# Attention's transposes one unit later, scores in two banks, and inputs loaded once or in place, in a hybrid encoder layer on one core

## The chip, the core and the metric

The kernel runs on one NeuronCore of a Trainium2 chip. The core has a matrix engine (TensorE, PE in the profile; its weight loads are PEld), a vector engine (VectorE, DVE), a scalar engine (ScalarE, ACT), GpSimd (POOL) and a sync engine (SyncE, SP). SP issues nearly all transfers of this kernel, and 16 DMA engines carry them out. Work on chip uses the SBUF (128 partitions); matmuls write into the PSUM, which here is cut into eight banks of 128 x 512 f32. The metric is the device time of one execution in microseconds (us): less is better. The engines run side by side, each through its own queue in order, and wait for each other through semaphores.

## What is computed

Two sequences (1024 and 2048 tokens of 1024 channels) each get 16 meta tokens in front and go through one encoder layer with shared weights. All of it is f32; the kernel splits every f32 operand of a large matmul into a high and a low part (`xh`, `xl`) and sums three products.

```python
xn = _rmsnorm(h, g_pre)
proj = xn @ w_in + b_in
na_q, na_k, na_v, na_z, ml_qk, ml_v, ml_z, ml_o, ml_g, mg = split(proj)
ya = (neighbourhood_attention(na_q, na_k, na_v, na_rpb) * silu(na_z)) @ w_a
yb = (mlstm_branch(ml_qk, ml_v, ml_g, ml_o, conv_w, head_g) * silu(ml_z)) @ w_b
ga, gb = split(sigmoid(mg))
y = (ga * ya + gb * yb) @ w_out
return h + _rmsnorm(y, g_post)
```

The attention puts the tokens on a grid of 64 columns. A query sees a window of 8 rows and 16 columns and the 16 meta tokens; the scores get a bias from a table, then softmax, then the product with v. There are 8 heads of 64 channels.

## The kernel before

TensorE's order is written out by hand: two generators yield pieces of work with a cost in us, and a small loop (`run`) takes dense pieces until they cover the cost of the sparse piece before. The order of the other engines' queues is set by a scheduler that plays the program through a timeline of its own, so an edit can move instructions there that the diff does not name.

*Dense* work (`dense`, following `PLAN`) is the input projection in half sequences and then six final blocks (`final`), each for 512 tokens. A final block has two halves. In the first, for each of eight column groups, 48 products take the branch outputs of the attention and the mLSTM, held as `yh` and `yl` (8 slices `k` of 128 channels, 0 to 3 attention, 4 to 7 mLSTM), with the merged weights; VectorE applies the gates (L1467, L1469) and the result is split into `mh` (L1470, ScalarE) and `mlo` (L1471, VectorE). In the second half 768 products form the output projection, which `final_out` normalises and adds to the input (L1571) during the next block. Weights come as `whi` and `wlo` through four buffers each (`wpump`, L243), issued when a buffer is free.

The branch outputs stand in DRAM (`YA`, `YB`). The generator `yload` fetches those of the next block: it is started in the last job of the projection (the first block) or in the second half of the block before (all others), and advanced one step at a time between TensorE's pieces. For each slice it waits until that slice is done (`self.done`), loads it into a buffer `yr` (L1418, 256 KB) of the pool tag `st`, which it shares with the gates' tiles and the projection's output tiles, and splits it two slices later: ScalarE copies it to `yh` (L1405), VectorE writes the rest to `yl` (L1406). The tiles `yh` and `yl` take their slots from the tags `xh` and `xl` (two each), as do `mh`, `mlo` and the projection's inputs.

*Sparse* work (`sparse`) is, in turn, the mLSTM and the attention (`na`) of the first sequence, then of the second (`STEPS`). Attention goes by blocks of eight grid rows, pairs of heads and heads: 16 heads' turns for the first sequence, 32 for the second, each with four *units*, one for each block of 16 query columns (`cb`). `na_prep` fetches and splits the inputs of the next head's turn in six steps between the units of this one: the queries `qr` (by `twice`, the same 64 rows to partitions 0 to 63 and again to 64 to 127), the keys `kr` (twice as well), the meta keys, the values `vr` and the gate `zt`. From `qr` it builds `stk`, whose lower 64 partitions are the high part of the queries and whose upper 64 the low part: ScalarE copies all 128 partitions (L824), VectorE overwrites the upper 64 with the difference (L827).

A unit passes through four stages, one for each yield in an iteration of `na`'s loop:

- `na_scores`: two products (L849, L850) into one PSUM bank `sc`; VectorE adds the bias and takes the extreme (L853, `mx`); ScalarE takes the exponential into `prb` (L857).
- `na_scale`: VectorE divides by the sum (L865, L866).
- `na_turn`: four transposes on TensorE (L874) into a bank `tr`; ScalarE and VectorE write the high and low part to `pts` (L876, L877).
- `na_out`: four products with v (L886) into a bank `sm`; ScalarE and VectorE add the three parts into `yg` (L890, L892). After the last unit of a pair of heads `yg` is gated (L894) and written to `YA` (L895), and the slice is marked done.

In iteration `u` the loop runs scores and scaling of unit `u`, the transposes of unit `u - 1` and the products with v of unit `u - 2`. The PSUM banks are `BANKS = dict(pj=3, tr=2, sc=1, sm=2)`: `pj` belongs to the dense work, `sc` holds the scores of attention and mLSTM, `sm` the products with v and several products of the mLSTM.

Of the kernel before, what the change touches and what calls it, by code (L numbers as in the profile page):

```python
# [9 lines left out]
F32 = mybir.dt.float32  # L10
# [7 lines left out]
P = 128  # L18
# [102 lines left out]
class K:  # L121
# [3 lines left out]
    def __init__(self, tc, ins, outs):  # L125
        self.tc, self.nc = tc, tc.nc
        self.xs = []
        self.i, self.o = ins, outs
        self.wreq, self.wraw, self.wrdy, self.wout = deque(), deque(), deque(), 0
        self.wseen, self.wkept, self.xkept = set(), {}, {}  # L130
        self.rwait = {}
        self.xput, self.turn, self.last = deque(), 0, None
        self.hold, self.early = deque(), True
# [601 lines left out]
    def na(self, s, rts):  # L735
# [3 lines left out]
        with tc.tile_pool(name=f"na{s}{rts[0]}", bufs=1, side="right", reuse_waits="tile") as np_:  # L739
# [18 lines left out]
            ready = {}  # L758
            for u in range(len(units) + 2):
                if u < len(units):  # L760
# [14 lines left out]
                yield A_NA  # L775
                if 1 <= u <= len(units):
                    self.na_turn(np_, ready[u - 1], rows)
                    if u < len(units) and cb >= 2:
                        next(prep, None)
                yield A_NA  # L780
                if u >= 2:
                    self.na_out(np_, ready.pop(u - 2), s)
                yield A_NA
# [9 lines left out]
    def na_prep(self, np_, s, rows, heads, j):  # L793
# [8 lines left out]
        qb = self.qB[hh]  # L802
        self.twice(qr, self.NQ[s][pr], h0, rt * 512)
        sv = stk.rearrange("p b t -> p (b t)")
# [18 lines left out]
        yield  # L823
        nc.scalar.activation(sv, qr, AF.Copy)  # L824
        yield
        nc.scalar.activation(qb[0:64], stk[0:64].bitcast(F32), AF.Copy)
        nc.vector.tensor_tensor(sv[64:128], qr[64:128], sv[64:128].bitcast(F32), op=ALU.subtract)  # L827
        yield
# [11 lines left out]
    def na_scores(self, np_, unit, rows):  # L840
# [5 lines left out]
        N, kc, g0 = ns * 32, KC0[cb], (5, 1, 0)[typ]  # L846
        sc = self.psum("sc", [P, 512])
        so = sc[:, :N].rearrange("p (a b) -> p a b", b=32)
        nc.tensor.matmul(so, stk[:, cb, :], kd[:, :ns, kc:kc + 32], start=True, stop=False)  # L849
        nc.tensor.matmul(so, qb[:, cb, :], self.kx[hh][:, :ns, kc:kc + 32], start=False, stop=True)  # L850
        pr_ = np_.tile([P, 512], F32, name="prb", bufs=2)
        mx = np_.tile([P, 1], F32, name="mx", bufs=3)
        nc.vector.tensor_tensor_reduce(  # L853
            out=so, in0=so, in1=gt[:, g0:g0 + ns, c0:c0 + 32],
            op0=ALU.add, op1=ALU.min, scale=-1.0, scalar=3.0e38, accum_out=mx)
        sm = np_.tile([P, 1], F32, name="sm", bufs=3)
        nc.scalar.activation(pr_[:, :N].rearrange("p (b a c) -> p b a c", b=4, c=8),  # L857
# [537 lines left out]
    def yload(self, s, b):  # L1395
# [5 lines left out]
        todo = deque()  # L1401

        def split():
            k, yr = todo.popleft()
            nc.scalar.activation(yh[:, k], yr, AF.Copy)  # L1405
            nc.vector.tensor_tensor(yl[:, k], yr, yh[:, k].bitcast(F32), op=ALU.subtract)  # L1406
            self.yk.add(k)

        for k in (4, 5, 6, 7, 0, 1, 2, 3):
            need = ("ml", s) if k > 3 else ("na", s, b, k)  # L1410
            if need not in self.done:
                while todo:
                    split()
                    yield
                while need not in self.done:
                    yield "wait"
            yr = fp.tile([P, n], F32, name="yr", tag="st", bufs=4)
            nc.sync.dma_start(yr, self.YA[s][b][k][:, :] if k < 4 else self.YB[s][k - 4][:, b * n:(b + 1) * n])  # L1418
            todo.append((k, yr))
            if len(todo) == 3:  # L1420
                split()
                yield
        while todo:
            split()
            yield

# [271 lines left out]
```

## Time and profile before

| | |
|---|---|
| time, median of 3 runs | 2843.53 us (2842.91 to 2847.38) |
| the profiled execution's own time | 2845.39 us |
| its span in the profile | 2843.6 us |
| its mean granted TensorE clock | 0.994 |
| DMA traffic over the span | 661.42 MB, 233 GB/s on average |

The page of the profile gives each engine's busy time and the costliest groups of instructions. A group's row reads: line, engine, operation, output <- inputs, count, busy time, mean of one, and the idle time before it with what ended it. Views of the trace narrow this: the waits (who waited for whom, in us, times and the longest), stretches (busy time of each engine between two points, with the granted clock as a share of full speed and the DMA engines' busy share), one line's instructions (shortest, median and longest duration in ns, then the first and last start), the timeline, and the chain of work that ended last. Times within the span count from its start. L numbers are lines of the kernel before.

### The profile page before, as it was taken

The page shows a single profiled execution, that of the slowest core. Times are in us where ns is not written, and L with a number is a line of the kernel's source. Part 1 is how long each engine was busy: PE and PEld are TensorE (multiplying, and loading weights), DVE is VectorE, ACT ScalarE, POOL GpSimd, SP SyncE. Part 2 cuts the span into 40 slices and gives each one's busy share as a digit, 9 for nine tenths or more (in the row PEclk, how much of TensorE's full clock was granted, in tenths as well). Part 3 has the DMA queues.
Part 4 walks back from the last instruction along what each step waited for, and adds up shares of the span by engine and source line. Part 5 has one row for each costly group of instructions (what it writes and reads, how often), then busy time and mean ns, then how long its engine had stood idle before and what let it go on. Part 6 is the DMA issues. An engine that isn't in the chain of part 4 may idle for free.

```text
span 2843.6 us, 49257 instructions
## 1 busy us (share of the span) xinstructions
PE 2795.7 (98%) x17312; PEld 2488.8 (88%) x17312; DVE 1796.3 (63%) x4931; ACT 1306.4 (46%) x3135; POOL 16.1 (1%) x103
## 2 busy tenths in 40 slices
PE   9999999999999999999999999999999999999998
PEld 8998898999899988888988888888888988889898
DVE  5233678576456654456667566474679888787854
ACT  5122546444444443355455555453455554545421
POOL 0000000000000000000000000000000000000000
PEclk9999999999999999999999999999999999999999
DMA  9554768765966554685656776656679999897875
GB/s 373 186 186 178 261 210 300 252 196 165 343 210 192 169 173 131 189 281 181 210 176 224 251 274 193 185 171 180 196 239 355 308 308 279 286 291 258 290 259 193
DMA packets 382120, 661.42 MB, mean 233 GB/s; under 512 B 51664, under 2 KB 200608, under 8 KB 381872
## 3 DMA queue, kind: packets, MB, share of 16 engines
q1 hardware_dynamic: 380752, 655.58, 69.7%
q0 software_dynamic: 1120, 2.69, 0.4%
q8 instruction: 137, 2.24, 0.3%
q14 instruction: 111, 0.91, 0.1%
HBM read 455.90 MB, written 202.22 MB: 231 GB/s over the span
## 4 chain that ended last, share of the span: by engine, by line
PE 85%; DMA 8%; DVE 5%; ACT 1%; issue 1%; SPq 0%; DVEq 0%; ACTq 0%
PE pj L155 15%; PE pj L156 14%; PE pj L157 14%; PE pj L577 6%; PE pj L578 6%; PE pj L579 6%; PE pj L1499 3%; PE pj L1497 3%; PE pj L1498 3%; PE sm L886 3%; PE tr L874 2%; DMA wlo<-wl 1%; DMA um<-ud 1%; PE sm L157 1%; PE sc L849 1%; PE sm L156 1%
## 5 line engine op out<-in xcount | busy, mean ns | idle before, releaser
L155 PE MATMUL pj<-xh,whi 128*128 128x512 f32 (+1 forms) x1792 | 705.7, 394 | 0.9 <-ACT whi L250 0.9
L156 PE MATMUL pj<-xl,whi 128*128 128x512 f32 (+1 forms) x1792 | 689.5, 385 | 0.1
L157 PE MATMUL pj<-xh,wlo 128*128 128x512 f32 (+1 forms) x1792 | 688.2, 384 | 0.3 <-DVE wlo L251 0.3
L577 PE MATMUL pj<-whi,xh 128*128 128x256 f32 (+3 forms) x1576 | 451.2, 286 | 4.4 <-DMA whi<-wh 2.9
L578 PE MATMUL pj<-wlo,xh 128*128 128x256 f32 (+3 forms) x1576 | 445.1, 282 | 0.8 <-DMA wlo<-wl 0.8
L579 PE MATMUL pj<-whi,xl 128*128 128x256 f32 (+3 forms) x1576 | 444.6, 282 | 0.0
L157 PEld LDWEIGHTS pj<-xh,wlo 128*128 128x128 f32 x1792 | 337.2, 188 | 72.1 <-DVE wlo L251 0.5
L155 PEld LDWEIGHTS pj<-xh,whi 128*128 128x128 f32 x1792 | 337.7, 188 | 60.5 <-ACT whi L250 1.7
L156 PEld LDWEIGHTS pj<-xl,whi 128*128 128x128 f32 x1792 | 338.0, 189 | 56.9 <-issue 1.0
L577 PEld LDWEIGHTS pj<-whi,xh 128*128 128x128 f32 (+1 forms) x1576 | 294.5, 187 | 6.4 <-DMA whi<-wh 3.1
L578 PEld LDWEIGHTS pj<-wlo,xh 128*128 128x128 f32 (+1 forms) x1576 | 294.3, 187 | 2.1 <-DMA wlo<-wl 1.1
L579 PEld LDWEIGHTS pj<-whi,xl 128*128 128x128 f32 (+1 forms) x1576 | 294.3, 187 | 0.9
L1497 PE MATMUL pj<-whi,mh 128*128 128x256 f32 x768 | 220.9, 288 | 4.2 <-DMA whi<-wh 2.4
L1499 PE MATMUL pj<-whi,mlo 128*128 128x256 f32 x768 | 217.5, 283 | 1.1 <-DVE mlo L1471 1.1
L1498 PE MATMUL pj<-wlo,mh 128*128 128x256 f32 x768 | 217.5, 283 | 0.1
L857 ACT ACTIVATE prb<-sc,mx 128x384 f32<-128x384 f32 (+2 forms) x192 | 119.8, 624 | 204.2 <-DVE mx L853 193.2
L877 DVE TENSOR_TENSOR pts<-tr,pts 96x512 fp32r<-96x512 f32 (+2 forms) x192 | 131.5, 685 | 75.8 <-ACT pts L876 74.3
L876 ACT ACTIVATE pts<-tr 96x512 fp32r<-96x512 f32 (+2 forms) x192 | 113.9, 593 | 114.8 <-PE tr L874 113.5
L155 PE MATMUL pj<-yh,whi 128*128 128x512 f32 x384 | 155.9, 406 | 0.0
L156 PE MATMUL pj<-yl,whi 128*128 128x512 f32 x384 | 152.2, 396 | 0.0
L157 PE MATMUL pj<-yh,wlo 128*128 128x512 f32 x384 | 152.2, 396 | 0.0
L1497 PEld LDWEIGHTS pj<-whi,mh 128*128 128x128 f32 x768 | 146.3, 190 | 6.5 <-ACT mh L1470 2.3
(271 smaller groups left out, 5049.4 us busy)
## 6 DMA issues: line engine op xcount, KB each, us to landing
whi<-wh SPq DMA_DIRECT2D x176, 512.0 KB
wlo<-wl SPq DMA_DIRECT2D x176, 512.0 KB
wraw<-wu SPq DMA_DIRECT2D x64, 512.0 KB
wh<-whi SPq DMA_DIRECT2D x64, 512.0 KB
wl<-wlo SPq DMA_DIRECT2D x64, 512.0 KB
gt<-st SPq DMA_DIRECT2D x96, 256.0 KB
tg<-gt SPq DMA_DIRECT2D x96, 256.0 KB
xt<-xt SPq DMA_DIRECT2D x32, 512.0 KB
```

The source lines that it names most:

```text
L155: mm(out, ah, bh, start=start, stop=False)
L156: mm(out, ah, bl, start=False, stop=False)
L157: mm(out, al, bh, start=False, stop=stop)
L577: nc.tensor.matmul(o, xh, wh, start=k == 0, stop=False)
L578: nc.tensor.matmul(o, xh, wl, start=False, stop=False)
L579: nc.tensor.matmul(o, xl, wh, start=False, stop=k == KT - 1)
L857: nc.scalar.activation(pr_[:, :N].rearrange("p (b a c) -> p b a c", b=4, c=8), sc[:, :N].rearrange("p (a b c) -> p b a c", b=4, c=8), AF.E ...
L876: nc.scalar.activation(pts[:ks, :, 0, :], pt[:ks], AF.Copy)
L877: nc.vector.tensor_tensor(pts[:ks, :, 1, :], pt[:ks], pts[:ks, :, 0, :].bitcast(F32), op=ALU.subtract)
L1497: nc.tensor.matmul(o, mh[:, k, xs], wh, start=k == 0, stop=False)
L1498: nc.tensor.matmul(o, mh[:, k, xs], wl, start=False, stop=False)
L1499: nc.tensor.matmul(o, ml[:, k, xs], wh, start=False, stop=k == KT - 1)
```

## The change

The change has four parts.

1. *Queries once.* `qr` is loaded only to partitions 0 to 63. ScalarE copies these 64 to `stk`, and VectorE takes the difference from partitions 0 to 63 and writes it to the upper 64.
2. *Transposes and v products one unit later.* In iteration `u` the loop now runs the transposes of unit `u - 2` and the products with v of unit `u - 3`, with one iteration more at the end. `prb` has three buffers and `mx` and `sm` (the sums) four.
3. *Scores in two banks in turn.* The scores of every other unit go to a bank of the tag `sm`, the rest to `sc` as before.
4. *Branch outputs in place.* `yload` loads a slice straight into its place in `yl`; ScalarE copies from there to `yh`, and VectorE subtracts in place. All slices that are done at the start are loaded at once; then come six empty steps, then one split a step. Slices that are not done yet are kept in `late` and loaded, with two empty steps, as soon as they are done.

```diff
@@ na
-            for u in range(len(units) + 2):
+            for u in range(len(units) + 3):
...
-                if 1 <= u <= len(units):
-                    self.na_turn(np_, ready[u - 1], rows)
+                if 2 <= u <= len(units) + 1:
+                    self.na_turn(np_, ready[u - 2], rows)
...
-                if u >= 2:
-                    self.na_out(np_, ready.pop(u - 2), s)
+                if u >= 3:
+                    self.na_out(np_, ready.pop(u - 3), s)
@@ na_prep
-        self.twice(qr, self.NQ[s][pr], h0, rt * 512)
+        nc.sync.dma_start(qr[0:64], self.NQ[s][pr][h0:h0 + 64, rt * 512:(rt + 1) * 512])
...
-        nc.scalar.activation(sv, qr, AF.Copy)
+        nc.scalar.activation(sv[0:64], qr[0:64], AF.Copy)
...
-        nc.vector.tensor_tensor(sv[64:128], qr[64:128], sv[64:128].bitcast(F32), op=ALU.subtract)
+        nc.vector.tensor_tensor(sv[64:128], qr[0:64], sv[0:64].bitcast(F32), op=ALU.subtract)
@@ na_scores
-        sc = self.psum("sc", [P, 512])
+        self.turns = not self.turns
+        sc = self.psum("sc" if self.turns else "sm", [P, 512])
...
-        pr_ = np_.tile([P, 512], F32, name="prb", bufs=2)
-        mx = np_.tile([P, 1], F32, name="mx", bufs=3)
+        pr_ = np_.tile([P, 512], F32, name="prb", bufs=3)
+        mx = np_.tile([P, 1], F32, name="mx", bufs=4)
@@ yload
+        def load(k):
+            nc.sync.dma_start(yl[:, k].bitcast(F32), self.YA[s][b][k][:, :] if k < 4 else self.YB[s][k - 4][:, b * n:(b + 1) * n])
+            todo.append(k)
+
         def split():
-            k, yr = todo.popleft()
-            nc.scalar.activation(yh[:, k], yr, AF.Copy)
-            nc.vector.tensor_tensor(yl[:, k], yr, yh[:, k].bitcast(F32), op=ALU.subtract)
+            k = todo.popleft()
+            nc.scalar.activation(yh[:, k], yl[:, k].bitcast(F32), AF.Copy)
+            nc.vector.tensor_tensor(yl[:, k], yl[:, k].bitcast(F32), yh[:, k].bitcast(F32), op=ALU.subtract)
             self.yk.add(k)
 
+        late = []
         for k in (4, 5, 6, 7, 0, 1, 2, 3):
-            need = ("ml", s) if k > 3 else ("na", s, b, k)
-            if need not in self.done:
-                while todo:
-                    split()
-                    yield
-                while need not in self.done:
-                    yield "wait"
-            yr = fp.tile([P, n], F32, name="yr", tag="st", bufs=4)
-            nc.sync.dma_start(yr, self.YA[s][b][k][:, :] if k < 4 else self.YB[s][k - 4][:, b * n:(b + 1) * n])
-            todo.append((k, yr))
-            if len(todo) == 3:
+            if (("ml", s) if k > 3 else ("na", s, b, k)) in self.done:
+                load(k)
+            else:
+                late.append(k)
+        for _ in range(6):
+            yield
+        while todo or late:
+            while late and (("ml", s) if late[0] > 3 else ("na", s, b, late[0])) in self.done:
+                load(late.pop(0))
+                for _ in range(2):
+                    yield
+            if todo:
                 split()
                 yield
-        while todo:
-            split()
-            yield
+            else:
+                yield "wait"
```

In the order of TensorE's instructions, which is fixed by hand, the counts and shapes of all products are the same before and after; the units of attention are shifted by one against each other as described. SP issues 48 transfers fewer. The queues of VectorE, ScalarE and SP are put in another order by the scheduler from the first attention on.

More of the change, by code (lines that the diff above doesn't have):

```diff
@@ L131, in __init__ @@
         self.rwait = {}
-        self.xput, self.turn, self.last = deque(), 0, None
+        self.xput, self.turn, self.last, self.turns = deque(), 0, None, False
         self.hold, self.early = deque(), True
@@ L855, in na_scores @@
             op0=ALU.add, op1=ALU.min, scale=-1.0, scalar=3.0e38, accum_out=mx)
-        sm = np_.tile([P, 1], F32, name="sm", bufs=3)
+        sm = np_.tile([P, 1], F32, name="sm", bufs=4)
         nc.scalar.activation(pr_[:, :N].rearrange("p (b a c) -> p b a c", b=4, c=8),
```

## The prediction

> **What bounds the kernel now.** I read the engine rows of the page first, then TensorE's waits, then where they fall, then one of them in order of time.
>
> ```profile
> PE 2795.7 (98%) x17312; PEld 2488.8 (88%) x17312; DVE 1796.3 (63%) x4931; ACT 1306.4 (46%) x3135; POOL 16.1 (1%) x103
> ```
>
> TensorE is busy for 2795.7 us of a span of 2843.6 us. The diff changes no matmul's count or shape, so nearly everything that it can win lies in the other 47.9 us. The waits of TensorE say whose they are (waited for, us in total, times, longest):
>
> ```profile
> PE tr L874 <- DVE prb L866: 12.3, 7, 3.3
> PE sc L849 <- ACT prb L857: 5.9, 4, 3.0
> PE pj L577 <- DMA whi<-wh: 2.9, 1, 2.9
> ...
> PE pj L1497 <- DMA whi<-wh: 2.4, 2, 1.6
> PE pj L1497 <- ACT mh L1470: 1.8, 1, 1.8
> ```
>
> The first two rows are the two that the change touches. Seven transposes waited for the scaled probabilities (12.3 us) and four score products for the exponentials to leave the only `sc` bank (5.9 us): 18.2 us. The stretches say where (start:end, length, then busy time and count of PE, PEld, DVE, ACT, POOL, then clock, DMA share, GB/s):
>
> ```profile
> 2100.00:2700.00 600.00, 579.31 (x3654) 519.46 (x3653) 497.93 (x1156) 311.40 (x731) 2.04 (x4) 0.99 0.92 299
> 710.00:1150.00 440.00, 436.34 (x2756) 394.50 (x2756) 245.02 (x626) 188.19 (x400) 1.74 (x16) 0.99 0.64 204
> ```
>
> Attention runs in both. In the first attention (second row) VectorE is busy 56% and TensorE loses 3.7 us in all. While the second attention runs beside the final blocks (first row), VectorE is busy 83%, the DMA engines 92%, and TensorE loses 20.7 us.
>
> One wait of the transposes, from the timeline (start, length, engine, line; TensorE's two rows first):
>
> ```profile
> 2641.17 0.64 PE L886 MATMUL sm<-pts,vt 104*128 104x256 f32 x4
> ...
> 2648.25 1.07 PE L874 MATMUL tr<-ident,prb 128*104 128x128 f32 x4 [3.32 <-DVE prb L866]
> ...
> 2644.36 0.26 DVE L892 TENSOR_TENSOR yg<-sm,yg 64x128 f32<-64x128 f32 x1
> ...
> 2645.74 1.41 DVE L1571 SCALAR_TENSOR_TENSOR yo<-yo,nwy,xres 128x512 f32<-128x512 f32 x2 [0.56 <-DMA xres<-x_sample]
> 2647.07 0.68 DVE L1469 TENSOR_TENSOR tg<-tg 128x512 f32<-128x512 f32 x1
> 2647.67 0.43 DVE L866 TENSOR_SCALAR prb<-prb,sm 128x416 f32<-128x416 f32 x1
> ```
>
> VectorE works its queue in order. The scaling (L866) stands behind a residual add (L1571) that waits for a transfer, and behind the final block's own operations. VectorE is not short of time over the stage (102 us free of 600), it is late in bursts, and the transposes are due too early to ride one out.
>
> **Transposes and v products one unit later.** A unit is one of the four column blocks of a head, and the stage holds:
>
> ```profile
> 2100.00:2700.00 600.00, 38.63 (x100) 19.09 (x100) 0.99 0.92 299
> ```
>
> This is the same stretch for the second score product (L850) alone: 100 units in 600 us, 6.0 us a unit. The transposes now come one unit, 6.0 us, later behind the same scaling. The longest wait is 3.3 us, so a burst like those of before is over 2.7 us ahead of the due time. Gain 12.3 us. The PSUM evacuation after the transposes and the v products move with them, so their distance stays.
>
> **Scores in two banks.** A score bank is now written again after two units and not one; for the scores in `sc` the longest wait of 3.0 us is covered by 6.0 more. Gain 5.9 us.
>
> **The clock.** Waits cost more than themselves. The transposes' waits in three stretches of a hundred us (from 2100, 2500 and 2200 on, one row of each), beside the longest of 3.0 and 3.3 us above (at 2573 and 2648); and then stretches of 20 us around the long ones:
>
> ```profile
> PE tr L874 <- DVE prb L866: 2.9, 2, 2.4
> PE tr L874 <- DVE prb L866: 2.8, 1, 2.8
> PE tr L874 <- DVE prb L866: 1.7, 1, 1.7
> ```
>
> ```profile
> 2155.00:2175.00 20.00, 17.09 (x78) 13.67 (x77) 17.31 (x37) 9.40 (x18) 0.00 (x0) 0.91 1.05 324
> 2515.00:2535.00 20.00, 17.21 (x79) 13.91 (x78) 16.64 (x37) 7.55 (x16) 0.51 (x1) 0.91 1.06 336
> 2560.00:2580.00 20.00, 17.04 (x119) 16.27 (x118) 15.46 (x34) 12.23 (x29) 0.00 (x0) 0.91 0.92 315
> 2640.00:2660.00 20.00, 16.68 (x78) 13.91 (x77) 17.66 (x41) 6.36 (x15) 0.00 (x0) 0.91 0.96 303
> 2280.00:2300.00 20.00, 18.29 (x92) 14.97 (x91) 18.16 (x41) 6.84 (x17) 0.00 (x0) 1.00 1.01 326
> ```
>
> The first four (waits of 2.4 to 3.3 us) have a granted clock of 0.91, the last (1.7 us) of 1.00. At 0.91, 20 us have lost 0.09 x 20 = 1.8 us. Four of them: 7.2 us, which goes with the waits. [...]
>
> **What the new place costs.** Two things can come back.
>
> The odd units' scores now share the two `sm` banks with the v products. In order of allocation that is product, scores, product, product, scores: half of the products and half of the scores must find the product of about one unit earlier evacuated, where a product used to have two units. In the burst above, a product issued at 2641.17 is out of its bank when L892 ends at 2644.62, 3.5 us later and inside 6.0; that is the lower end, nothing. The upper end is the nearest row of a wait at one unit's distance, the scores' own 5.9 us with one clock loss, 7.7 us. Half of the units are affected, so I take half of 5.9: 3.0 us.
>
> The v product keeps its distance to its operand, and the pause that TensorE made at the transposes no longer holds it back. Its smallest margin in the trace:
>
> ```profile
> 2195.76 0.68 DVE L877 TENSOR_TENSOR pts<-tr,pts 128x512 fp32r<-128x512 f32 x1
> ...
> 2197.63 0.60 PE L886 MATMUL sm<-pts,vt 128*128 128x256 f32 x3
> ```
>
> The operand is ready at 2196.44, 1.2 us ahead. If each of the four largest transposes' waits (3.3, 2.8, 2.4, 1.7) met such a margin, 2.1 + 1.6 + 1.2 + 0.5 = 5.4 us would return; if VectorE has caught up by then, nothing. I take the middle, 2.7 us.
>
> **Queries once.** 48 of these transfers go, one for each head:
>
> ```profile
> qr<-nq SPq DMA_DIRECT2D x96, 128.0 KB
> ```
>
> That is 48 issues fewer on SP's queue and 6.3 MB. TensorE waited for no query, so I count nothing; the upper end is a gain of 3 us, the weights' wait of 2.9 us in the third row of the waits, which falls where attention starts and the queue is crowded. ScalarE's copy and VectorE's subtraction stay one operation each over 512 columns.
>
> **Branch outputs in place.** The 48 loads, copies and subtractions (below, of 128x512 f32, 256 KB each) remain in the same shapes:
>
> ```profile
> L1406 DVE TENSOR_TENSOR yl<-yr,yh x48: 673/684/694, 2101.5 to 2730.9; 128x512 fp32r<-128x512 f32 x48
> ```
>
> New is that up to eight loads (2.1 MB) are issued together, then six steps pass, then one split a step; before, loads ran three ahead. They write a slot of `yl` whose last reader, the block before, is past, so SP does not wait long for it. 2.1 MB at 299 GB/s is 7.0 us in front of the next weights. Weights have four buffers, so a transfer is issued two to three units ahead. Eight of the 48 copies below belong to a block and fill the first half of its time; 48 span five and a half blocks, so a block takes about 118 us, a unit of weights 7.4 us and the lead is 15 to 22 us. The second row is the slowest weight transfer that I saw in the chain of waits:
>
> ```profile
> L1470 ACT ACTIVATE mh<-tg x48: 612/632/636, 2140.1 to 2788.2; 128x512 fp32r<-128x512 f32 x48
> ...
> 2300.01 8.80 DMA whi<-wh
> ```
>
> 8.8 + 7.0 = 15.8 us just fits. I count nothing; the case that it doesn't is a rival.
>
> The tail: the last attention row is now finished one unit later, with 84 output products left behind it instead of 156 (one every 0.12 us by the first two rows below: 9.9 us of cover). From the last v product's evacuation (third row) to the end of the last split, which the row of L1406 has starting at 2730.9, the trace has 7.3 us:
>
> ```profile
> 2729.73 0.28 PE L1499 MATMUL pj<-whi,mlo 128*128 128x256 f32 x1
> 2729.85 0.28 PE L1497 MATMUL pj<-whi,mh 128*128 128x256 f32 x1
> ...
> 2724.27 0.60 DVE L892 TENSOR_TENSOR yg<-sm,yg 64x128 f32<-64x128 f32 x2 [1.27 <-ACT yg L890]
> ```
>
> and the last eighth of that block's inputs is read only after 21 products of 512 columns more. So nothing; without that cover the last block would start some 7 us late.
>
> **Sum.** 12.3 + 5.9 + 7.2 - 3.0 - 2.7 = 19.7 us off the profiled execution's 2845.4 us, which stands 1.9 us above the median of the three runs (2843.5). From the median: 2824 us. Its own range is 2815 to 2831: nothing given back and 3 us for the queries, or both costs of the new place at their upper ends (7.7 + 5.4 us).
>
> **The rivals.**
>
> VectorE takes the time back. It is at 83%, and with TensorE earlier by 20 us the same bursts meet the next consumers: v products, final blocks' `pj` banks, `mh` and `mlo` at the head of the output products, which already show 1.8 us. For it speaks the 83%; against it, that 102 us of VectorE are free and each burst is shorter than the new distance. If three quarters of the 25.4 us return, 6 us remain: 2837 us.
>
> The burst of loads makes the kernel slower. From the point where a weight transfer behind the eight loads takes more than the lead of 15 us and upward, TensorE waits in each of the six final blocks. With a DMA share of 0.92 to 1.06 that is near. Three us and a clock loss of 1.8 us in each block are 29 us: 2843.5 - 19.7 + 29 = 2853 us. Against it: only 2.4 us of waits for weights are seen now in the final blocks.
>
> The change doesn't do what it says: VectorE's order is set anew by due times, and scaling that is due later may be queued later, so that the transposes are late as before. Then only the scores' 5.9 us and one clock loss go: 2836 us. Against it: the unit's own scores to exponential chain has no later due time.
>
> More than I forecast: the weights' waits (2.9 and 2.4 us) and those of `mh` (1.8 us) go too, with one clock loss each for the first and last, for less traffic and a VectorE that is ahead, some 10 us: 2814 us.
>
> **How the numbers follow.** Forecast 0.58, VectorE 0.14, due times 0.07, loads 0.15, more 0.06. The measurement of this kernel can tell 0.2%, 5.7 us, from no change: below 2837.8 is faster. Forecast and more are faster, and a third of the 0.21 of the two middle cases: 0.71. The rest of these is no change (0.14), and the loads are slower: 0.15. The range reaches from the extra gain to a mild form of the burst: 2814 to 2846.
>
> **What would show it.** Right: the rows of transposes waiting for L866 and scores waiting for L857 gone or under 3 us together, the busy time of PE unchanged but for the clock, no 20 us stretch at 0.91 between 2100 and 2700. Bank sharing wrong: waits of scores or of the v products' first matmul for VectorE's L892. VectorE: new waits at L886, L155 or L1497 of the same total. Loads: L1497 or L155 waiting for weights by more than 2.4 us in total. Queries: fewer bytes by 6.3 MB. The prediction fails if these waits go and the span does not follow them.

## The result and the profile after

The changed kernel takes 2836.33 us (median of 7 runs, 2834.41 to 2840.43), the kernel before on the same chip 2847.38 us (7 runs, 2842.91 to 2854.93). The ratio is 0.9961 with a 95% interval of 0.9943 to 0.9979: faster, by about 11 us. The forecast was 19.7 us less. Direction and range held, the size did not. The profiled execution took 2834.41 us, with a span of 2832.6 us against 2843.6 us before, so the profiles show the same 11.0 us.

Engine rows of the page, after (busy time, share of the span, instructions):

```profile
PE 2790.1 (99%) x17312; PEld 2484.0 (88%) x17312; DVE 1791.9 (63%) x4931; ACT 1307.6 (46%) x3135; POOL 16.2 (1%) x103
```

TensorE's busy time fell by 5.6 us (2795.7 to 2790.1) with the counts unchanged: that is the granted clock, 0.996 on average against 0.994. What remains of the span beside it fell by 5.4 us, from 47.9 to 42.5. The waits of TensorE, after (waited for, us in total, times, longest; lines of this kernel are one to six higher than before):

```profile
PE sm L887 <- ACT prb L858: 6.1, 5, 2.4
PE sm L157 <- DVE ktl L1155: 5.7, 5, 1.9
PE sm L887 <- DVE yg L893: 5.6, 4, 3.0
...
PE sm L850 <- DVE yg L893: 2.5, 4, 1.4
PE pj L1503 <- DMA whi<-wh: 2.1, 2, 1.4
PE sm L850 <- DVE sm L866: 1.9, 1, 1.9
...
PE sm L887 <- ACT kd L829: 1.2, 1, 1.2
```

The rows of the transposes and of the scores waiting for `sc`, 18.2 us, are gone. In their place stand 17.3 us on the two `sm` banks: 12.9 us at the v products (L887: 6.1 + 5.6 + 1.2) and 4.4 us at the odd units' scores (L850: 2.5 + 1.9). The other 4.5 us of the smaller idle time are little rows that came and went: waits for `mh` (1.8), `mlo` (1.1), `kf` (1.2) and two mLSTM rows of products into the score bank (2.6 and 0.8) are gone, one for `ktl` grew from 2.6 to 5.7.

The second attention (start:end, length, busy time and count of PE, PEld, DVE, ACT, POOL, then clock, DMA share, GB/s):

```profile
2100.00:2700.00 600.00, 582.77 (x3719) 523.45 (x3718) 497.93 (x1173) 313.37 (x744) 2.04 (x4) 0.99 0.91 296
```

TensorE loses 17.2 us of the 600 where it lost 20.7. One of the new waits in order of time, from the timeline of the changed kernel:

```profile
2519.67 0.68 DVE L878 TENSOR_TENSOR pts<-tr,pts 128x512 fp32r<-128x512 f32 x1
...
2521.84 0.69 ACT L858 ACTIVATE prb<-sm,mx 128x512 f32<-128x512 f32 x1 [2.22 <-DVE mx L854]
...
2522.68 0.74 PE L887 MATMUL sm<-pts,vt 128*128 128x256 f32 x4 [1.59 <-ACT prb L858]
```

The operand `pts` was ready at 2520.35, more than two us ahead. The product started 0.15 us after the exponential of the scores *of the same iteration* had ended (2522.53): it had been given the `sm` bank in which those scores stood. In every odd iteration a unit's scores and its product both need an `sm` bank and only two exist, so the product must wait either for those scores or for the product of the iteration before. All ten waits of the products (0.2 to 3.0 us) fall in odd iterations and end 0.14 to 0.15 us after the one or the other: five after the exponential of those scores (6.1 us), five after L893 of the product before. The rows that name `kd` (L829) and the sums `sm` (L866) are of the second kind: there too L893 ended 0.15 us before the start, and the instruction named happened to end a little later.

### The profile page after: what moved, and what is told of

Same layout as the page of the kernel before. It is cut to its first block, busy times and chain, and to the rows that moved or that the text cites. A ratio compares the mean times of both kernels' runs of the same rounds, so it can differ in the third digit from the quotient of the medians.

```text
span 2832.6 us, 49099 instructions
## 1 busy us (share of the span) xinstructions
PE 2790.1 (99%) x17312; PEld 2484.0 (88%) x17312; DVE 1791.9 (63%) x4931; ACT 1307.6 (46%) x3135; POOL 16.2 (1%) x103
## 2 busy tenths in 40 slices
DMA packets 378278, 655.11 MB, mean 231 GB/s; under 512 B 50896, under 2 KB 199840, under 8 KB 378032
## 4 chain that ended last, share of the span: by engine, by line
PE 85%; DMA 7%; DVE 5%; ACT 1%; issue 1%; SPq 0%; DVEq 0%; ACTq 0%
PE pj L155 15%; PE pj L156 15%; PE pj L157 15%; PE pj L577 6%; PE pj L578 6%; PE pj L579 6%; PE pj L1503 3%; PE pj L1505 3%; PE pj L1504 3%; PE sm L887 3%; PE tr L875 2%; PE sm L157 1%; DMA wlo<-wl 1%; PE sm L156 1%; PE sm L155 1%
## 5 line engine op out<-in xcount | busy, mean ns | idle before, releaser
L1504 PEld LDWEIGHTS pj<-wlo,mh 128*128 128x128 f32 x768 | 147.0, 191 | 1.7
```

Of the source, the lines that this page charges most:

```text
L1504: nc.tensor.matmul(o, mh[:, k, xs], wl, start=False, stop=False)
```

## The experiments

The runs stand here by question, not in order of time, so an expectation can name a result that is told further down. Each ratio is against runs of the kernel before on the same chip and need not be the quotient of two medians. The spans of single profiled executions scatter by more than the effects looked for, so ratios decide about time and profiles about places. "The attention's waits" are those that begin at 2100 us or later.

### Each part alone

Part 1 alone on the kernel before:

```diff
-        self.twice(qr, self.NQ[s][pr], h0, rt * 512)
+        nc.sync.dma_start(qr[0:64], self.NQ[s][pr][h0:h0 + 64, rt * 512:(rt + 1) * 512])
...
-        nc.scalar.activation(sv, qr, AF.Copy)
+        nc.scalar.activation(sv[0:64], qr[0:64], AF.Copy)
```

> The kernel before with part 1 alone (queries loaded once). Parts 1 and 4 together cost 0.65% when attention is not shifted. Theory A (the loads in place do it, by a burst of splits): this kernel is within 0.2% of before and the transposes wait near 12 us. Theory B (the queries do it, by the new order of the queues): it is slower by 0.4% or more, with 20 us or more of waits of the transposes.

Measured: ratio 1.0013 (0.9996 to 1.0029), no change that can be told. Transposes waited 17.5 us in 8 places in its profile.

Part 4 alone on the kernel before:

```diff
-            nc.scalar.activation(yh[:, k], yr, AF.Copy)
-            nc.vector.tensor_tensor(yl[:, k], yr, yh[:, k].bitcast(F32), op=ALU.subtract)
+            nc.scalar.activation(yh[:, k], yl[:, k].bitcast(F32), AF.Copy)
+            nc.vector.tensor_tensor(yl[:, k], yl[:, k].bitcast(F32), yh[:, k].bitcast(F32), op=ALU.subtract)
...
+        for _ in range(6):
+            yield
```

> The kernel before with part 4 alone (branch outputs loaded in place, all at once). Theory A: slower by 0.4 to 0.7%, with some 20 us or more of waits of the transposes for L866, the added ones around the splits before each final block. Theory B: within 0.2% of before. If neither alone is slower, the two add up only through the order that the scheduler finds for them together.

Measured: ratio 1.0026 (1.0011 to 1.0040), slightly slower. Transposes waited 20.5 us in 10 places.

Parts 1 and 4 together (both edits above):

> Parts 1 and 4 of the change alone (queries once, branch outputs in place), attention's order and banks as before. If these two are neutral, as the prediction has it, the time is that of before within 0.2% (5.7 us) and TensorE's waits of the transposes for L866 and of the scores for the exponential stay near 18 us. If loading all slices at once lets the splits run in a burst that holds up ScalarE and VectorE, those waits grow and the time is above that of before by 3 us or more. If they are a gain of their own, it is below by more than 3 us.

Measured: ratio 1.0065 (1.0042 to 1.0088), 18 us slower. Its waits:

```profile
PE tr L874 <- DVE prb L866: 24.1, 12, 4.6
PE sc L849 <- ACT prb L857: 7.6, 4, 5.3
...
PE pj L1502 <- DMA whi<-wh: 2.8, 2, 2.2
```

Weights are waited for by little more than before in the final blocks (2.8 and, for `wlo`, 0.8 us against 2.4), so delayed weights are not what costs 18 us. The transposes' row doubled (12.3 to 24.1): with these edits the scaling comes later, and as long as the transposes are due early, TensorE pays. Neither part alone explains it, with 0.13% that can't be told from nothing and 0.26%; how the two add up to 0.65% is open.

Part 2 alone:

```diff
-                    self.na_turn(np_, ready[u - 1], rows)
+                    self.na_turn(np_, ready[u - 2], rows)
...
-                    self.na_out(np_, ready.pop(u - 2), s)
+                    self.na_out(np_, ready.pop(u - 3), s)
```

> The kernel before with part 2 alone (transposes and v products one unit later, prb three times). If the shift is the part that gains, as the run with one score bank suggests (0.9973 with parts 1, 2 and 4, against 1.0065 with 1 and 4), the transposes' waits go to under 1 us, the scores still wait for the exponential by 6 to 13 us, and the time is 0.2 to 0.5% below before. If it gains only by repairing what parts 1 and 4 cost, it is within 0.2% of before.

Measured: ratio 0.9985 (0.9973 to 0.9996), some 4 us. Its waits:

```profile
PE sc L849 <- ACT prb L857: 17.1, 11, 5.3
```

The transposes no longer wait, but the scores' wait for their one bank grew from 5.9 to 17.1 us. What was won at one place came back at the next place with little distance.

Part 3 alone:

```diff
-        sc = self.psum("sc", [P, 512])
+        self.turns = not self.turns
+        sc = self.psum("sc" if self.turns else "sm", [P, 512])
```

> The kernel before with part 3 alone (scores in the sc bank and in an sm bank in turn). Question: does sharing the two sm banks cost anything by itself, while TensorE still pauses at the transposes and the distance from the last product with v to its evacuation is 3.2 us as before? If the order of allocation alone costs (two sm banks are too few for one unit's scores and two products), TensorE waits for sm banks by 10 us or more, as in the changed kernel (17.3 us), and the time is about that of before or slower, ratio 1.000 to 1.004. If those waits come from the lag that the shift brings, TensorE waits for sm banks by less than 6 us, the scores' 5.9 us go, the transposes keep 10 to 15 us, and the ratio is 0.996 to 0.9995.

Measured: ratio 1.0007 (0.9991 to 1.0023). The waits came as the second expectation had them, the time as the first: the scores' wait for `sc` went, and nothing was gained. Its waits:

```profile
PE tr L875 <- DVE prb L867: 14.0, 9, 3.4
PE pj L1498 <- ACT mh L1471: 5.9, 1, 5.9
PE sm L887 <- ACT prb L858: 4.1, 4, 1.6
...
PE sm L887 <- ACT yh L1406: 0.8, 1, 0.8
PE sm L887 <- DVE yg L893: 0.8, 1, 0.8
```

At the v products the sharing gave back 5.7 us (4.1 + 0.8 + 0.8) of the 5.9 it saved; the 5.9 us for `mh` are one wait of this execution. With the shift in place it costs 17.3 us. The transposes lie between a unit's scores and its product with v in TensorE's order; here they still stand for 14.0 us, and in that time banks come free.

### The changed kernel with one part taken out

Without part 3, all scores in `sc` again:

```diff
-        self.turns = not self.turns
-        sc = self.psum("sc" if self.turns else "sm", [P, 512])
+        sc = self.psum("sc", [P, 512])
```

> The changed kernel with the scores always in sc: parts 1, 2 and 4. Theory 1 (the 17 us of new waits come from scores and v products sharing the two sm banks): the v products' waits (17 us of new waits, 12.9 of them at the v products) go to under 3 us, the scores' waits for the exponential come back with about 6 us, and the time is 4 to 10 us below the changed kernel. Theory 2 (VectorE is late whatever the banks are): the v products wait as in the changed kernel and the score waits come on top, so the time is 3 us or more above the changed kernel.

Measured: ratio 0.9973 (0.9962 to 0.9984), which can't be told from the changed kernel's 0.9961. The waits of the v products went but for 0.9 us, as the first theory had it. In their place the scores waited 12.7 us in 13 places for `sc`, twice what that theory gave them and not far from what the two `sm` banks cost in the changed kernel (17.3).

Without part 4, the loads of the kernel before:

```diff
-            nc.scalar.activation(yh[:, k], yl[:, k].bitcast(F32), AF.Copy)
+            nc.scalar.activation(yh[:, k], yr, AF.Copy)
```

> The changed kernel with the loading of the branch outputs as before (through st, three loads ahead, splits apart). Theory 3 (the burst of splits, behind loads that land late, holds ScalarE and VectorE in the output products): the three waits of v products in those halves (1.3, 2.6 and 3.0 us) go, and with two clock losses the time is 5 to 10 us below the changed kernel. Theory 1 (only the banks): the waits keep their total of 17 us within 4 us and the time stays within 3 us.

Measured: ratio 0.9976 (0.9963 to 0.9989), and the same waits at the same places:

```profile
PE sm L887 <- ACT prb L858: 8.2, 6, 2.4
PE sm L850 <- DVE yg L893: 7.0, 3, 4.3
```

So part 4 is not the source of the new waits, and the rival of the burst of loads falls a second time. That does not clear late loads as such: they stand in SyncE's queue with part 4 and without it.

### More banks

Scores, transposes and v products of the changed kernel take the banks `sc`, `tr`, `sm`, `tr`, `sm` in turn, so that a bank is written again after five pieces:

```diff
+    def bank(self):
+        self.turns += 1
+        return self.psum(("sc", "tr", "sm", "tr", "sm")[self.turns % 5], [P, 512])
...
-        av = self.psum("sm", [P, 512])
+        av = self.bank()
```

> The changed kernel with the five banks sc, tr, sm, tr, sm given in turn to scores, transposes and v products, so that each bank comes up again after five uses, one and two thirds of a unit. Theory 1 (sharing of two banks within one unit): scores' and v products' waits fall from 17 us to under 5 us, and with the clock losses the time is 12 us or more below the changed kernel (about 2824 us). Theory 2 (VectorE late whatever the banks are): waits of the same sum come at the v products for pts or at the transposes, and the time is that of the changed kernel within 3 us.

Measured: ratio 0.9951 (0.9934 to 0.9968). The five banks are waited for by 0.2 us in all. Now the products' operand is:

```profile
PE sm L890 <- DVE pts L881: 8.8, 3, 3.4
```

The first theory wanted 12 us less than the changed kernel, the second the same time within 3 us with waits at `pts`. The second comes nearer: the two intervals overlap, and the lateness met the next buffer.

The same on the kernel before with part 2 (parts 1 and 4 left out), the edit being those of part 2 and of the banks above:

> The kernel before with part 2 and the five banks in turn, without parts 1 and 4. If the banks were the cause of the new waits and parts 1 and 4 give nothing, the time is at or below that of the changed kernel with five banks (0.995 of before), with no wait for a bank and less than 9 us for pts. If parts 1 and 4 help once attention is shifted, it is above 0.997.

Measured: ratio 0.9948 (0.9928 to 0.9967), the same as with parts 1 and 4, whose cost is hidden once the distances are large. The products' operand is waited for by 0.9 us here. The waits have moved again, to the projection's banks and `mlo`:

```profile
PE pj L1501 <- DVE yo L1529: 4.6, 2, 4.1
...
PE pj L1503 <- DVE mlo L1475: 3.6, 2, 2.9
```

Four buffers in turn (operand of the transposes, score bank, `sm` bank, projection bank) have now been the one that TensorE stands before. That left the question of what makes VectorE and ScalarE late.

### What is late

With the distances grown, both engines also run later behind TensorE: over some 100 units of the second attention the time from the start of a unit's last v product to the end of its evacuation averages 3.2 us before and 3.8 us after. My next theory was that this mean lag makes the new waits, since a pause of TensorE had also been time for VectorE to catch up. The multiplication by the reciprocal of the sum (L866) is 46.3 us of VectorE's work between 2100 and 2700. It goes to ScalarE, on the kernel before and on the changed kernel:

```diff
-        nc.vector.tensor_scalar(pr_[:, :N], pr_[:, :N], sm, None, op0=ALU.mult)
+        nc.scalar.activation(pr_[:, :N], pr_[:, :N], AF.Copy, scale=sm)
```

> The kernel before, only the multiplication by the reciprocal of the sum (L866) goes from VectorE to ScalarE. It takes 46 us of the 600 us from 2100 on off VectorE (83% to 75%) and puts some 50 to 60 us on ScalarE (52% to 61%). If lateness of VectorE is what TensorE waits for, the transposes' waits (12.3 us) fall to 6 us or less and the time falls by 6 to 15 us, ratio 0.995 to 0.998. Rival: ScalarE's own queue (exponentials, copies of four other kinds) is as bursty; the transposes wait as before, now for ScalarE, and the exponentials behind a late multiplication hold the only bank of the scores longer: ratio 0.999 to 1.004.

Measured on the kernel before: ratio 0.9943 (0.9921 to 0.9965), at least as much as the whole change. Its attention's waits:

```profile
PE sc L849 <- ACT prb L857: 7.2, 4, 2.7
...
PE tr L874 <- ACT prb L866: 1.8, 3, 1.0
```

The transposes' waits went from 12.3 to 1.8 us with no distance added. Little of them reappeared: the scores' row went from 5.5 us (of its 5.9, those after 2100) to 7.2. The multiplication itself takes longer there (0.64 against 0.44 us in the median), but it comes sooner when VectorE is behind: from the end of the exponential to the end of the multiplication the slowest ten of some 100 take 3.0 us or more against 4.9, the longest 4.4 against 6.5.

> The changed kernel with the same move of the multiplication to ScalarE. If what remains (17.3 us of waits for sm banks) is the lag of VectorE and ScalarE behind a TensorE that no longer pauses, 46 us less on VectorE should bring the distance from the last product with v to its evacuation from 3.8 us to 3.4 or less and the waits for sm banks to 8 us or less: ratio to the kernel before 0.990 to 0.994. Rival (the banks' order sets the waits, whatever VectorE does): waits stay at 14 to 20 us, ratio 0.995 to 0.998. Second rival: ScalarE becomes the late one (the evacuation begins with ScalarE's copy into yg), waits grow over 20 us, ratio 0.998 to 1.002.

Measured on the changed kernel: ratio 0.9965 (0.9949 to 0.9981), no gain over 0.9961. The lag from product to evacuation fell to 3.2 us as the theory wanted, but 11.9 us of waits for `sm` banks stayed, more than the theory's 8 and less than the first rival's 14, and 1.6 us for the operand came up. The time is what the first rival gave. So the mean lag can explain a part of the waits at most, and nothing of the time; as the cause that theory falls. The longest wait shows another one (timeline; in brackets idle time before and what ended it):

```profile
2317.05 0.40 PE L850 MATMUL sm<-kd,stk 128*128 128x512 f32 x1
...
2320.62 0.63 ACT L1410 ACTIVATE yh<-yl 128x512 fp32r<-128x512 f32 x1 [5.98 <-DMA yl<-yb]
...
2324.89 1.66 ACT L1410 ACTIVATE yh<-yl 128x512 fp32r<-128x512 f32 x3
...
2326.57 0.69 ACT L858 ACTIVATE prb<-sm,mx 128x512 f32<-128x512 f32 x1
...
2327.40 1.22 PE L887 MATMUL sm<-pts,vt 128*128 128x256 f32 x4 [4.00 <-ACT prb L858]
```

ScalarE stood 6 us at the head of its queue before a copy of a branch output whose load had not landed, then had everything behind it to do at once. The exponential of scores written at 2317 ended at 2327.3, and the product of that iteration, placed in that bank, waited 4.0 us. The longest wait of the changed kernel, 3.0 us at 2450.6, has the same start; its timeline:

```profile
2444.55 1.30 ACT L1410 ACTIVATE yh<-yl 128x512 fp32r<-128x512 f32 x2 [4.75 <-DMA yl<-yb]
```

The five banks and part 2 on the kernel before, with the multiplication on ScalarE (the three edits above):

> The shift and five banks in turn on the kernel before (no other part), with the multiplication on ScalarE: the candidate for the best. Without that move this version waits for projection banks (4.6), mlo (3.6) and tg (2.0), all VectorE's, at a ratio of 0.9948. If VectorE's lag is what is left, these fall below 5 us together and the ratio is 0.990 to 0.993. If ScalarE becomes the late one, waits for mh, for pts and for the exponentials take their place with 8 us or more and the ratio is 0.994 to 0.998.

Measured: ratio 0.9932 (0.9907 to 0.9958). Waits for a projection bank remain (`yo` of VectorE, 8.4 us in 2 places), and ScalarE did not become the late one. Within the intervals this is the same as the multiplication's move alone: where lateness is removed, the added distance brings little.

### Loads of the branch outputs from another queue

These loads stand in SyncE's queue, in which weight loads wait for a free buffer. SyncE's waits in the changed kernel, from 2100 to 2740:

```profile
SPq L243 <- PE pj L1505: 72.2, 23, 12.2
```

What is queued behind such a weight load stands with it, up to 12.2 us. GpSimd, busy 1% of the span, now issues the branch outputs' loads. In the changed kernel:

```diff
-            nc.sync.dma_start(yl[:, k].bitcast(F32), self.YA[s][b][k][:, :] if k < 4 else self.YB[s][k - 4][:, b * n:(b + 1) * n])
+            nc.gpsimd.dma_start(yl[:, k].bitcast(F32), self.YA[s][b][k][:, :] if k < 4 else self.YB[s][k - 4][:, b * n:(b + 1) * n])
```

> The changed kernel, only the loads of the branch outputs (L1405) are issued by GpSimd and not by SyncE. In the changed kernel the longest wait for an sm bank (3.0 us at 2450) follows a ScalarE that stood 4.8 us at the head of its queue before a copy whose load was late, and then copied several slices in a row. If that late load is what makes the remaining waits, ScalarE's waits for these loads (16.7 us from 2100 on) fall below 5 us, the waits for sm banks in the attention (14 us of the 17.3, the rest not counted here) to 7 us or less, and the ratio to the kernel before is 0.991 to 0.994. Rival (two banks are too few in the odd units, whatever the loads do): the ScalarE waits go, those for sm banks stay at 10 us or more, ratio 0.995 to 0.998.

Measured: ratio 0.9949 (0.9930 to 0.9967). The attention's waits:

```profile
PE pj L1503 <- DMA whi<-wh: 6.1, 3, 3.3
PE sm L887 <- ACT prb L858: 4.7, 4, 1.9
PE pj L1504 <- DMA wlo<-wl: 2.5, 3, 1.0
PE sm L850 <- DVE yg L893: 2.1, 3, 1.4
PE sm L850 <- DVE sm L866: 1.8, 1, 1.8
PE sm L887 <- DVE yg L893: 1.1, 2, 0.7
PE sm L887 <- ACT pts L877: 0.8, 1, 0.8
PE sm L850 <- ACT yh L1410: 0.6, 1, 0.6
```

The two longest waits of the changed kernel (3.0 at 2450, 2.4 at 2329) are gone and the `sm` banks cost 11.1 us, not 17.3. ScalarE's waits for these loads fell from 16.7 to 8.6 us from 2100 on, not below 5: SyncE's queue was a part of their lateness, not all of it. So by these two profiles some 6 us of the waits came from late loads and 11 us stay with the two banks: the rival's numbers, mostly. In time the step is not told apart (0.9949 against 0.9961, the intervals overlap). New are 6.5 us more of waits for weights (6.1 + 2.5 against 2.1), now that these loads no longer queue behind them.

The same on the kernel before (`yr`, L1418), alone and with the multiplication on ScalarE:

> The kernel before, only its loads of the branch outputs (L1418) are issued by GpSimd. If late loads make VectorE late in the kernel before too, the transposes' waits (12.3 us) fall to 6 us or less and the ratio is 0.994 to 0.998. If the place of the multiplication in VectorE's queue makes them, as its move to ScalarE suggests (ratio 0.9943), they stay at 9 to 15 us and the ratio is 0.998 to 1.002.

Measured: ratio 0.9959 (0.9943 to 0.9975). The transposes' row stayed at 11.9 us, as the second theory said, and yet the time fell. In its profile 7.4 of 10.4 us are TensorE's busy time (2788.3 us), that is, the granted clock (0.997 against 0.994). A part of the rest can be placed: the scores' row fell from 5.9 to 3.5 us, and the wait of 2.6 us for `qh` in the mLSTM, beside which the kernel before has a clock of 0.83 (1880 to 1900), is gone. Why, is open.

> The kernel before with both: the multiplication on ScalarE (L866) and the loads (L1418) from GpSimd. With the multiplication alone 7.8 us of waits of scores for their bank remain. If ScalarE's standing before late loads (23.5 us from 2100 on in that version) makes them, they fall below 3 us and the ratio is 0.990 to 0.993; if not, they stay at 5 to 9 us and the ratio is 0.993 to 0.996.

Measured: 2819.49 us against 2841.58 us, ratio 0.9919 (0.9902 to 0.9937): the fastest kernel of the study, with none of the change's four parts in it. Its interval lies below that of the changed kernel. It is what the first expectation gave: the scores' waits for their bank fell from 7.8 to 1.7 us, and ScalarE's for the loads from 23.5 to 7.4. All its attention's waits:

```profile
PE pj L1497 <- DMA whi<-wh: 4.6, 4, 1.9
PE pj L1498 <- DMA wlo<-wl: 1.6, 2, 0.9
PE sc L849 <- ACT prb L857: 1.2, 2, 0.6
PE pj L1497 <- DVE yo L1525: 0.7, 1, 0.7
PE tr L874 <- ACT prb L866: 0.7, 2, 0.4
```

```profile
2100.00:2700.00 600.00, 593.53 (x3828) 535.55 (x3826) 471.95 (x1088) 381.18 (x863) 26.36 (x48) 1.00 0.95 303
```

The one score bank of the kernel before, and transposes one unit behind, are enough once little is late: 1.9 us for both, where 17.8 us (12.3 and 5.5) were lost from 2100 on.

Everything together, that is the changed kernel with five banks, the multiplication on ScalarE and the loads from GpSimd:

> The candidate with everything: the changed kernel with five banks in turn, the multiplication on ScalarE and the loads of the branch outputs from GpSimd. If the three causes (bank distance, the multiplication's queue, late loads) add up, waits of TensorE from 2100 on fall below 8 us in all and the ratio is 0.989 to 0.992. If what they give is the same lateness counted three times, the ratio stays at 0.992 to 0.996, with the waits at projection banks or mlo.

Measured: ratio 0.9934 (0.9915 to 0.9954). The gains do not add up. What TensorE waits for is now mostly weights:

```profile
PE pj L1506 <- DMA whi<-wh: 7.1, 4, 3.4
```

## Why the prediction was right in direction and wrong in size

**Transposes, 12.3 us.** Right: the row is gone, here and in the kernel with part 2 alone. As a gain it did not stand by itself: part 2 alone brings some 4 us (ratio 0.9985), because 11.2 us came back at the score bank.

**Scores in two banks, 5.9 us.** The row for `sc` is gone as said. The argument that the new distance covers the longest wait held only for the units that stay in `sc`.

**The clock, 7.2 us.** TensorE's busy time fell by 5.6 us, which is near, but by luck. The four stretches that I priced do run at 1.00 now (the one from 2515 is the last row). But two stretches of the changed kernel lose clock, the first two rows, which hold the waits of 2.4 and 3.0 us:

```profile
2320.00:2340.00 20.00, 17.44 (x127) 16.68 (x126) 16.61 (x39) 12.90 (x33) 0.00 (x0) 0.91 0.72 238
2440.00:2460.00 20.00, 16.96 (x115) 16.36 (x114) 14.82 (x32) 12.50 (x30) 0.00 (x0) 0.83 1.07 331
2515.00:2535.00 20.00, 18.41 (x95) 15.37 (x94) 17.98 (x39) 8.98 (x20) 0.51 (x1) 1.00 1.04 363
```

At 0.91 and 0.83 they lose 1.8 and 3.4 us of 20, 5.2 us together. I had counted no loss in new places, and I had overlooked two old ones. In the kernel before:

```profile
2440.00:2460.00 20.00, 17.37 (x126) 16.53 (x126) 14.01 (x34) 11.03 (x28) 0.00 (x0) 0.91 1.02 290
1880.00:1900.00 20.00, 16.62 (x71) 14.07 (x72) 13.50 (x43) 11.14 (x27) 0.00 (x0) 0.83 0.72 240
```

and from 1880 to 1900 in the changed one:

```profile
1880.00:1900.00 20.00, 20.00 (x106) 16.88 (x104) 13.74 (x54) 9.74 (x26) 0.00 (x0) 1.00 0.88 304
```

So the final blocks gave 7.2 - 5.2 + 1.8 = 3.8 us, and another 3.4 us came from a place outside them that I had not priced: the mLSTM of the second sequence, where the two rows of 2.6 and 0.8 us had stood. Read off stretches, which hold waits too, that makes 7.2 us; in busy time it is 5.6. The waits of the eight profiled versions without part 2 hold rows of the mLSTM's products into the score bank for `qh` or `ql`, 0.8 to 4.2 us in all; those of the ten with it list none (five of these lists end at rows of 0.4 to 1.0 us). So this gain goes with the shift; by what path, is open.

**What the new place costs, 3.0 + 2.7 us.** This is the step that failed. Sharing the `sm` banks cost 17.3 us, not 3.0, and more than the 7.7 us I had as its upper end; the products' operand cost nothing. I listed the order of allocation (product, scores, product, product, scores) and the right waits, but priced them by the scores' wait in a trace in which TensorE still stood 12.3 us at the transposes. Part 3 alone shows that this price was fair for the old order: 5.7 us. With the pauses at the transposes gone, late moments of VectorE and ScalarE met the tightest buffer that was left. I had bounded the operand by exactly this transfer of waits (the four longest transposes' waits meeting a margin of 1.2 us) and did not apply it to the banks, whose margin is smaller: in the burst that I quoted a product left its bank after 3.5 us of 6.0, but an odd unit's product may get the bank of its own iteration's scores. Where the banks were made plentiful, the operand's price turned up after all in one version (8.8 us), but not in the other (0.9).

In the prediction's own terms: 12.3 + 5.9 + 5.6 - 17.3 - 0 = 6.5 us, and 4.5 us of rows that I had not priced, make the 11.0 us measured.

**Queries once and branch outputs in place, nothing.** Right behind the shift (five banks: 0.9951 with them, 0.9948 without), wrong by themselves: 1.0065 together. Traffic fell by 6.3 MB, as said:

```profile
DMA packets 378278, 655.11 MB, mean 231 GB/s; under 512 B 50896, under 2 KB 199840, under 8 KB 378032
```

**The rivals.** The burst of loads delaying the weights did not come: 2.1 us of waits for weights in the final blocks against 2.4. Due times did not undo the change. As a time two rivals came close, "VectorE takes the time back" with 2837 us and the due times with 2836, against 2836.33. That is partly luck: both count from 2843.5 us, the median of three runs, and the seven runs beside the changed kernel have 2847.38, so they stood for gains of 6.5 and 7.5 us where 11 were measured. "VectorE" was right that the same bursts meet the next consumers, and it named the v products among them; that part of the time comes back was its whole point. But as it was argued, through VectorE's 83%, it is not what the runs show: taking 46 us off VectorE in the changed kernel changed nothing in its time, 6.1 of the 17.3 us ended with an exponential of ScalarE, and five banks took these waits away.

**What the runs settle and what they don't.** Shown: waits move from buffer to buffer as each is given distance; in the changed kernel the place is the two `sm` banks in odd iterations; the multiplication on ScalarE alone brings as much as the shift with five banks (0.9943 and 0.9948), and with the loads from GpSimd more than the change (0.9919 against 0.9961). By one profile each, about 6 of the 17.3 us come from late loads of the branch outputs. Not settled: what makes the other 11 us of evacuations and exponentials late, how parts 1 and 4 add up, how the shift helps the mLSTM, and how much of a ratio such as 0.9959 with unchanged waits of the transposes is the clock alone.

## What to carry to other kernels

The waits that late engines caused here were not removed by giving one consumer more distance: they moved to the next (with part 2 alone 12.3 us went at the transposes and 11.2 us came at the score bank). Before pricing the gain, list the next buffers by their margins and let the same burst meet each of them, with the pauses that you remove taken out of the trace. Ask first why the producer is late: here one multiplication moved to another queue, and loads taken out of a queue in which they stood behind waiting weight loads, brought twice as much as four edits that moved due times and banks (0.9919 against 0.9961). Test a compound change part by part as well: here two parts that looked free cost 0.65% without the shift.

## What the runs showed of the hardware

In the traces of the kernel before and of the changed kernel a lower clock often stands beside a wait of TensorE of a few us, but the wait's length does not decide. Over stretches of 20 us of the kernel before the granted clock was 1.00 beside a wait of 1.7 (from 2280) and beside one of 1.8 us (from 2320), 0.91 beside waits of 1.8 and 0.8 us (from 2440), 0.91 beside one of 3.0 (from 2560) and one of 3.3 us (from 2640), and 0.83 beside 2.6 and 0.8 us (from 1880). In the changed kernel it was 1.00 beside 1.6 (from 2515), 0.91 beside 2.4 and 0.2 (from 2320) and 0.83 beside 3.0 us (from 2440). So the 1.8 to 3.4 us that a stretch at 0.91 or 0.83 lost cannot be put on a wait by its length.

One execution is a poor witness for a few us: the 27 runs of the kernel before on one chip went from 2832.62 to 2854.71 us, and the version with part 2 and five banks was profiled in an execution of 2823.72 us while its median is 2834.07.

Loads of 256 KB issued by GpSimd cost it little (in the fastest version 26.4 us busy in 600 for 48 instructions, against 2.0 us for 4 in the kernel before), but more waits for weights came with them: 8.6 us in the final blocks against 2.1 in the changed kernel, and 3.7 against 2.4 in the kernel before, with the same traffic (655.12 against 655.11 MB, and 661.42 MB in both).
